# Row passes two fetches behind, every second one-hot on VectorE, and 64 expert chunks ahead instead of 80

## The chip, the cores and the metric

The kernel runs on one core of a Trainium2 chip. The metric is the device time in microseconds (us) from the start to the end of one execution; a median over several executions is quoted. The engines are called TensorE (PE in the rows, PEld for its weight loads), VectorE (DVE), ScalarE (ACT), GpSimd (POOL) and SyncE (SP, which issues most DMAs). Each engine runs its own list of instructions strictly in order and waits on semaphores for the others.

## The reference, cut to what matters

One layer of a decoder trunk over 512 tokens of width 2048, in float32. A mixer (sparse attention and a Mamba-2 scan) comes first and is not touched. After it stands PEER, a retrieval over 16384 one-neuron experts: each token picks 16 experts for each of 8 heads, 128 in all, and adds up what they give.

```python
v1, i1 = lax.top_k(s1, 16); v2, i2 = lax.top_k(s2, 16)      # s1, s2: scores of 128 + 128 keys
best, pos = lax.top_k(cand, 16)                             # cand: the 256 sums v1 + v2
eidx = take_along_axis(i1 * 128 + i2, pos); gate = softmax(best)
act = gelu(einsum('td,tkd->tk', h, u_tab[eidx]))            # 128 rows of u for each token
ffn = einsum('tk,tkd->td', act * gate, v_tab[eidx])         # 128 rows of v for each token
```

`u_tab` and `v_tab` are 16384 x 2048, 128 MB each.

## The kernel before, in words

The 512 tokens of PEER are split between two ways of computing the same thing.

- **352 tokens the dense way.** All experts are computed for these tokens, and a matrix G of gates, zero for experts that a token did not pick, is multiplied in. The experts come in 128 chunks of 128. A *u chunk* (`uchunk`, L826) loads 1 MB of `u` in two halves. `wsplit` (L241) brings each half (`wr`), lets ScalarE round it (`wh`, L248) and VectorE take the rest (`wl`, L249); the pools have 3 buffers of each. TensorE then does 48 matmuls of 352 columns (L253 to L255, three for a product), and ScalarE applies gelu (`ac`, L835). A *v group* (`vgroup`, L1057) is the same with `v` for 8 chunks: 16 halves, and VectorE adds each result into `outT` (L1075, L1077).
- **160 tokens by rows.** GpSimd fetches, in 320 steps of 1 MB, one row of 2048 for each of 128 partitions (`rows`, L950, 3 buffers). VectorE makes a *row pass* over each: a dot product with h for the 160 rows of `u` (L955), then a multiply-add into `facc` for the 160 of `v` (L964, L971). `gather_step` (L945) writes the fetch and its pass one behind the other. `pace` (L977) sets when the fetches go: each u chunk counts one unit of work, each of the 16 halves of a v group half a unit, 256 in all; for each unit 333/256 = 1.3 fetches become due, and each waits for the instruction that ended the unit.

The order of the stages, with the lines that matter:

1. *Routing.* VectorE finds the top 16 (`route`, L855). After each of the 8 heads `go_ahead` (L984) writes 4 u chunks (`NA_TOPK`) whose `ac` goes to DRAM (`ascr`) for later.
2. *G.* For 11 blocks of 32 tokens, 8 banks of 4 tokens each: VectorE makes `oa` (L1015), the one-hot of the first key; ScalarE makes `ob`, the one-hot of the second key times the gate, in two activations (L1020, L1021; 8 buffers); TensorE multiplies them (L1022), and ScalarE copies the bank out to `stg` (L1023). After each block `go_ahead` writes `NA_G` = 4 u chunks, and after the last block what is left of the `NA` = 80.
3. *Groups.* The 16 groups of 8 chunks. `wgroup` (L1035) makes the weights of v: for chunks below `NA` it loads `ac` back from `ascr`, the others are computed there. `vgroup` follows. The list `order` puts a group that is still to be computed before one that is ready: with 80 ahead 10, 0, 11, 1, ... 15, 5, and then 6, 7, 8, 9.
4. *End.* The last groups' sums, the 160 tokens' transposes, the final norm.

What the kernel writes is not what an engine runs. A scheduler lays each engine's list out from the written order: of the instructions that it takes to be ready at a time it takes the first written, and `wsplit`'s two go ahead of all others (`tc.high_priority`). So the place of a row pass in VectorE's list is set by both.

Of the kernel before, what the change touches and what calls it, by code (L numbers as in the profile page):

```python
# [13 lines left out]
AF = mybir.ActivationFunctionType  # L14
ALU = mybir.AluOpType
# [10 lines left out]
NB = 384 - ND  # L26
QB = 128 // NB
GRP = 8
NA = 80
NA_TOPK = 4  # L30
NA_G = 4
UAB = 4
WB = 12
ADA_SSM = (0, 0, 1, 1, 2, 2, 2, 2)
# [121 lines left out]
def build(tc, nc, I, out, dbg=None, stop=None):  # L156
    dbg = dbg or {}
    es = ExitStack()
    V, S, PE, G, SP = nc.vector, nc.scalar, nc.tensor, nc.gpsimd, nc.sync
# [20 lines left out]
    iota = cst[:, C_IOTA:C_IOTA + 128]  # L180
# [35 lines left out]
    for hf in range(2):  # L216
        ct = adp.tile([128, 1024], F32, name="ct", tag="at", bufs=3)
        sl = slice(1024 * hf, 1024 * hf + 1024)
# [4 lines left out]
    def after_(ins, first):  # L223
        if first is not None:
            tc.add_manual_dep(ins.ins, first.ins.name,
                              mybir.DependencyInfo(mybir.DependencyClass.Sync, mybir.DependencyReason.DATA), reason="pace")
# [114 lines left out]
    with ExitStack() as sx:  # L341
# [80 lines left out]
        for g in range(2):  # L422
# [7 lines left out]
            for c in range(4):  # L430
                sl = slice(128 * c, 128 * c + 128)
# [7 lines left out]
        for p in range(8):  # L439
# [17 lines left out]
            for j in range(2):  # L457
                for c in range(4):
                    V.tensor_scalar(M[:, j, c], R[:, j, 128 * c:128 * c + 128], acst[:, c, 2 * p + j:2 * p + j + 1], 0.0,
                                    op0=ALU.subtract, op1=ALU.min)  # L460
# [13 lines left out]
            for c in range(4):  # L474
                sl = slice(128 * c, 128 * c + 128)
# [6 lines left out]
                if c < 3:  # L482
# [5 lines left out]
                    else:  # L488
                        for j in range(2):
                            V.scalar_tensor_tensor(Sn[:, 64 * j:64 * j + 64], St[:, 64 * j:64 * j + 64],  # L490
                                                   eal[:, j, c:c + 1], su[:, 64 * j:64 * j + 64],
                                                   op0=ALU.mult, op1=ALU.add)
# [28 lines left out]
    with ExitStack() as sx:  # L521
# [10 lines left out]
        with tc.tile_pool(name="mlp", bufs=1) as mp:  # L532
# [9 lines left out]
            for c0, n in ((0, 512), (512, 128)):  # L542
# [3 lines left out]
                                       op0=ALU.mult, op1=ALU.add)  # L546
            SP.dma_start(rvscr, rv.unsqueeze(1).to_broadcast([16, 128, 640]))
            for which in range(2):
# [33 lines left out]
                if which == 0:  # L582
# [3 lines left out]
                    for k in range(2):  # L586
                        sl = slice(NCMP * k, NCMP * k + NCMP)
# [43 lines left out]
        for h in range(NH):  # L631
# [4 lines left out]
            if h == 14:  # L636
                mH, mL = act_tiles()
                for k in range(0, 8, 2):
                    m = st.tile([128, 1024], F32, name="wr", tag="wr")
                    SP.dma_start(m.rearrange("p (a b) -> p a b", a=2), yscr[k:k + 2].rearrange("a p b -> p a b"))  # L640
                    for c in range(2):
                        sl = slice(T * c, T * c + T)
# [20 lines left out]
            for br in range(3):  # L663
                for i in range(4):
# [8 lines left out]
                    if br == 0:  # L673
                        bias = TB[:, 415 - 128 * i:415 - 128 * i + 16 * (n - 1) + 1:16]
                    else:
                        bias = TB[:, 384 - 128 * i:384 - 128 * i + n]
                    V.tensor_tensor_reduce(out=P, in0=sps[:, :n], in1=bias, scale=1.0, scalar=3e38, op0=ALU.add,
                                           op1=ALU.min, accum_out=mn[:, ki:ki + 1])
# [141 lines left out]
    I2T = ixp.tile([128, ND], F32, name="I2T")  # L820
# [121 lines left out]
    steps = [("u", 0, sl) for sl in range(128)] + [("u", 1, sl) for sl in range(NB)] + \  # L942
        [("v", 0, sl) for sl in range(128)] + [("v", 1, sl) for sl in range(NB)]

    def gather_step(s, after):  # L945
        nonlocal facc, faccb
        side, grp, sl = steps[s]
        rows = gp.tile([128, D], F32, name="rows", tag="rows", bufs=3)
        ei = eidxb if grp else eidx
        ins = G.indirect_dma_start(out=rows, out_offset=None, in_=I["un"] if side == "u" else I["vn"],  # L950
                                   in_offset=bass.IndirectOffsetOnAxis(ap=ei[:, sl:sl + 1], axis=0))
        after_(ins, after)
        c = 128 * grp + sl
        if side == "u":
            V.scalar_tensor_tensor(rows, rows, 1.0, h2b if grp else h2t, op0=ALU.mult, op1=ALU.mult,  # L955
                                   accum_out=dots[:, c:c + 1])
            n = NB if grp else 128
            if sl == n - 1:
                gs_ = slice(128 * grp, 128 * grp + n)
                S.activation(wgt[:, gs_], dots[:, gs_], AF.Gelu_apprx_tanh)  # L960
                V.tensor_tensor(wgt[:, gs_], wgt[:, gs_], ggateb if grp else ggate, op=ALU.mult)
        elif sl == 0:
            f = gp.tile([128, D], F32, name="facc", tag="faccb" if grp else "facc")
            V.tensor_scalar(f, rows, wgt[:, c:c + 1], None, op0=ALU.mult)  # L964
            if grp:
                faccb = f
            else:
                facc = f
        else:
            f = faccb if grp else facc  # L970
            V.scalar_tensor_tensor(f, rows, wgt[:, c:c + 1], f, op0=ALU.mult, op1=ALU.add)  # L971
# [5 lines left out]
    def pace(units, after):  # L977
        nonlocal gdone, work
        work += units
        while gdone < min(len(steps), G0 + (GEND - G0) * work / total):  # L980
            gather_step(gdone, after)
            gdone += 1

    def go_ahead(n):  # L984
        for _ in range(n):
# [22 lines left out]
    with tc.tile_pool(name="gstage", bufs=1, side="right") as sp:  # L1008
        for tq in range(ND // 32):
            stg = sp.tile([128, 128, 32], F32, name="stg", tag="stg", bufs=2)  # L1010
            for t4 in range(8):
                gb = next(gbank)()
                t0 = 32 * tq + 4 * t4
                oa = sp.tile([128, 4, 128], F32, name="oa", tag="oa", bufs=3)
                V.tensor_tensor(oa, iota.unsqueeze(1).to_broadcast([128, 4, 128]),  # L1015
                                I1T[:, t0:t0 + 4].unsqueeze(2).to_broadcast([128, 4, 128]), op=ALU.is_equal)
                for k in range(4):
                    t = t0 + k
                    ob = sp.tile([128, 128], F32, name="ob", tag="ob", bufs=8)
                    S.activation(ob, iota, AF.Square, bias=I2N[:, t:t + 1])  # L1020
                    S.activation(ob, ob, AF.Relu, scale=GTN[:, t:t + 1], bias=GTT[:, t:t + 1])  # L1021
                    PE.matmul(gb[:, 128 * k:128 * k + 128], ob, oa[:, k], start=True, stop=True)  # L1022
                S.copy(stg[:, :, 4 * t4:4 * t4 + 4].rearrange("p a t -> p t a"),  # L1023
                       gb.rearrange("p (t a) -> p t a", t=4))
            SP.dma_start(gscr[tq], stg)
            go_ahead(NA_G)
    go_ahead(NA)
# [115 lines left out]
```

## Time and profile before

| what | us |
|---|---|
| median of 3 runs | 3595.86 (3570.61 to 3595.88) |
| the profiled execution | 3587.35 |
| its span, first to last instruction | 3585.6 |
| TensorE busy | 3210.6 (90%) |
| VectorE busy | 2685.9 (75%) |
| ScalarE busy | 1526.0 (43%) |
| GpSimd busy | 489.7 (14%) |

The profile gives instructions with start and duration, and for each wait of an engine what released it. Busy is the sum of durations without overlaps. Matmuls are pipelined, so their durations overlap and the step from one start to the next is what one costs; the same holds, less strongly, for ScalarE and VectorE. PEclk is the share of TensorE's full clock (2.4 GHz) that was granted. DMA share is the mean busy share of the 16 DMA engines. A bank here is the work on 4 tokens of G: one `oa`, four `ob`, four products, one copy.

### The profile page before, as it was taken

Reading aid. Unit: us, or ns where it says so; the run is one execution under the profiler, and the core shown is the slowest. Engines: PE = TensorE matmul, PEld = TensorE weight load, DVE = VectorE, ACT = ScalarE, POOL = GpSimd, SP = SyncE. Lnnn points to the kernel's source line nnn. Section 1 sums busy time; section 2 is a strip of 40 time slices with the busy share of each in tenths; the row PEclk is TensorE's granted clock in tenths of the full one; section 3 lists DMA queues with packets and bytes.
Section 4 is the critical chain, followed back from the end, with each engine's and each line's share of the span. In section 5 each row is a group of like instructions: output and inputs, shape, how many; then the busy total and the mean of one; then the engine's idle time right before and its main releaser. Section 6 shows DMA issues by size and latency. Waiting matters only on the chain. (4 is left out here: it accounts for less than half of the span.)

```text
span 3585.6 us, 48243 instructions
## 1 busy us (share of the span) xinstructions
PE 3210.6 (90%) x18025; PEld 2942.0 (82%) x18025; DVE 2685.9 (75%) x4567; ACT 1526.0 (43%) x2775; POOL 489.7 (14%) x324
## 2 busy tenths in 40 slices
PE   5999679999899999868888999999898989988897
PEld 3777568878677999858777999989898989988897
DVE  8888479977777999725554577777777768777786
ACT  3443247962432434498777432323222232322222
POOL 0000000000000112101011122322322222232220
PEclk9999889999899999969899999999999999999999
DMA  9647884238522888736676788898888888798884
GB/s 345 245 160 236 187 270 137 76 107 283 191 88 93 283 299 328 274 125 241 251 275 249 294 317 299 309 320 321 303 289 313 307 301 310 280 319 303 309 313 144
DMA packets 292666, 905.02 MB, mean 252 GB/s; under 512 B 24064, under 2 KB 89856, under 8 KB 249264
## 3 DMA queue, kind: packets, MB, share of 16 engines
q1 hardware_dynamic: 246352, 566.39, 47.0%
q0 software_dynamic: 46080, 335.56, 24.3%
q8 instruction: 141, 2.31, 0.3%
q14 instruction: 93, 0.76, 0.1%
HBM read 845.46 MB, written 56.39 MB: 252 GB/s over the span
## 5 line engine op out<-in xcount | busy, mean ns | idle before, releaser
L248 ACT CAST wh<-wr 128x1024 fp32r<-128x1024 f32 x646 | 676.1, 1049 | 1196.2 <-DMA wr<-in_ut_dram 251.1
L249 DVE TENSOR_TENSOR wl<-wr,wh 128x1024 fp32r<-128x1024 f32 x646 | 786.9, 1221 | 194.9 <-ACT wh L248 180.9
L255 PE MATMUL mm<-dh,wl 128*128 128x352 f32 x2048 | 682.9, 333 | 44.4 <-DVE wl L249 44.0
L253 PE MATMUL mm<-dh,wh 128*128 128x352 f32 x2048 | 678.2, 331 | 1.0 <-ACT wh L248 1.0
L254 PE MATMUL mm<-dl,wh 128*128 128x352 f32 x2048 | 675.6, 330 | 0.0
L971 DVE SCALAR_TENSOR_TENSOR facc<-rows,wgt,facc 128x2048 f32<-128x2048 f32 x158 | 371.3, 2350 | 172.4 <-DMA rows<-in_vn_dram,eidx 147.5
L255 PEld LDWEIGHTS mm<-dh,wl 128*128 128x128 f32 x2048 | 395.1, 193 | 55.2 <-DVE wl L249 54.8
L950 POOL DMA_INDIRECT rows<-in_un_dram,eidx x128 | 159.4, 1245 | 2049.9 <-DMA wr<-in_ut_dram 1183.1
L253 PEld LDWEIGHTS mm<-dh,wh 128*128 128x128 f32 x2048 | 394.3, 193 | 1.6 <-ACT wh L248 1.6
L254 PEld LDWEIGHTS mm<-dl,wh 128*128 128x128 f32 x2048 | 394.7, 193 | 0.0
L955 DVE SCALAR_TENSOR_TENSOR rows<-rows,h2t 128x2048 f32<-128x2048 f32 x128 | 292.6, 2286 | 131.2 <-DMA rows<-in_un_dram,eidx 131.2
L253 PE MATMUL mm<-ah,wh 128*128 128x512 f32 x864 | 344.0, 404 | 5.5 <-DVE rr__7022 L287 3.1
L254 PE MATMUL mm<-al,wh 128*128 128x512 f32 x864 | 346.0, 401 | 0.0
L255 PE MATMUL mm<-ah,wl 128*128 128x512 f32 x864 | 345.0, 400 | 0.0
L950 POOL DMA_INDIRECT rows<-in_vn_dram,eidx x128 | 220.7, 1724 | 630.8 <-ACT ac L835 198.9
L236 DVE SCALAR_TENSOR_TENSOR at<-at,cond 128x1024 f32<-128x1024 f32 x192 | 231.4, 1221 | 41.6 <-DMA at<-in_ada_dram 41.1
L253 PEld LDWEIGHTS mm<-ah,wh 128*128 128x128 f32 x864 | 164.8, 191 | 40.9 <-issue 5.5
L254 PEld LDWEIGHTS mm<-al,wh 128*128 128x128 f32 x864 | 164.8, 191 | 34.2 <-issue 3.0
L255 PEld LDWEIGHTS mm<-ah,wl 128*128 128x128 f32 x864 | 164.3, 190 | 34.7 <-issue 3.0
L1021 ACT ACTIVATE ob<-ob,GTT,GTN 128x128 f32<-128x128 f32 x352 | 155.2, 486 | 0.0
L1015 DVE TENSOR_TENSOR oa<-cst,I1T 128x512 f32<-128x512 f32 x88 | 59.8, 690 | 121.2 <-PE t L1022 52.1
L1020 ACT ACTIVATE ob<-cst,I2N 128x128 f32<-128x128 f32 x352 | 121.6, 393 | 0.0
(2961 smaller groups left out, 6588.1 us busy)
## 6 DMA issues: line engine op xcount, KB each, us to landing
wr<-in_ut_dram SPq DMA_DIRECT2D x256, 512.0 KB, 5.5
wr<-in_vn_dram SPq DMA_DIRECT2D x256, 512.0 KB, 6.3
at<-in_ada_dram SPq DMA_DIRECT2D x192, 512.0 KB, 5.7
wr<-in_win_dram SPq DMA_DIRECT2D x54, 512.0 KB, 4.9
gscr<-stg SPq DMA_DIRECT2D x11, 2048.0 KB, 12.5
gt<-gscr SPq DMA_DIRECT2D x32, 704.0 KB, 8.8
wr<-in_wo_dram SPq DMA_DIRECT2D x32, 512.0 KB, 5.2
wr<-in_wq_dram SPq DMA_DIRECT2D x32, 512.0 KB, 3.8
```

The lines of the kernel that those rows point to most:

```text
L236: V.scalar_tensor_tensor(at, at, 1.0, cond[:, sl], op0=ALU.mult, op1=ALU.mult, accum_out=acc[:, hf, k:k + 1])
L248: S.copy(hi[:, :n], raw[:, :n])
L249: V.tensor_tensor(lo[:, :n], raw[:, :n], hi[:, :n].bitcast(F32), op=ALU.subtract)
L253: PE.matmul(acc, wh, ah, start=start, stop=False)
L254: PE.matmul(acc, wh, al, start=False, stop=False)
L255: return PE.matmul(acc, wl, ah, start=False, stop=stop)
L950: ins = G.indirect_dma_start(out=rows, out_offset=None, in_=I["un"] if side == "u" else I["vn"], in_offset=bass.IndirectOffsetOnAxis(ap=ei ...
L955: V.scalar_tensor_tensor(rows, rows, 1.0, h2b if grp else h2t, op0=ALU.mult, op1=ALU.mult, accum_out=dots[:, c:c + 1])
L971: V.scalar_tensor_tensor(f, rows, wgt[:, c:c + 1], f, op0=ALU.mult, op1=ALU.add)
L1015: V.tensor_tensor(oa, iota.unsqueeze(1).to_broadcast([128, 4, 128]), I1T[:, t0:t0 + 4].unsqueeze(2).to_broadcast([128, 4, 128]), op=ALU.is ...
L1020: S.activation(ob, iota, AF.Square, bias=I2N[:, t:t + 1])
L1021: S.activation(ob, ob, AF.Relu, scale=GTN[:, t:t + 1], bias=GTT[:, t:t + 1])
```

## The change

Three edits. `gather_step` is cut into `fetch` and `use_rows`, and a row pass is written only when two more fetches have been written (`LAG` = 2). Of the four `ob` of a bank the first and third are made by VectorE in one instruction, an `is_equal` with one per-partition scalar and a `mult` with another; the second and fourth stay on ScalarE. And `NA` falls from 80 to 64 with `NA_G` from 4 to 3, so 16 u chunks move from the G stage into the groups, whose order becomes 8, 0, 9, 1, ... 15, 7.

```diff
-NA = 80
+NA = 64
 NA_TOPK = 4
-NA_G = 4
+NA_G = 3
+LAG = 2
...
-    def gather_step(s, after):
-        nonlocal facc, faccb
+    fetched = []
+
+    def fetch(s, after):
         side, grp, sl = steps[s]
         rows = gp.tile([128, D], F32, name="rows", tag="rows", bufs=3)
...
         after_(ins, after)
+        fetched.append((side, grp, sl, rows))
+
+    def use_rows():
+        nonlocal facc, faccb
+        side, grp, sl, rows = fetched.pop(0)
         c = 128 * grp + sl
...
         while gdone < min(len(steps), G0 + (GEND - G0) * work / total):
-            gather_step(gdone, after)
+            fetch(gdone, after)
             gdone += 1
+            if len(fetched) > LAG:
+                use_rows()
+        while gdone == len(steps) and fetched:
+            use_rows()
...
-                    S.activation(ob, iota, AF.Square, bias=I2N[:, t:t + 1])
-                    S.activation(ob, ob, AF.Relu, scale=GTN[:, t:t + 1], bias=GTT[:, t:t + 1])
+                    if k % 2:
+                        S.activation(ob, iota, AF.Square, bias=I2N[:, t:t + 1])
+                        S.activation(ob, ob, AF.Relu, scale=GTN[:, t:t + 1], bias=GTT[:, t:t + 1])
+                    else:
+                        V.tensor_scalar(ob, iota, I2T[:, t:t + 1], GTT[:, t:t + 1], op0=ALU.is_equal, op1=ALU.mult)
```

How the lists of the engines change is shown at three places. The number at a row's start is its place in the engine's list, L the line of that kernel (the changed one has 13 or 14 lines more there).

ScalarE in the G stage, two banks (`stg` is the copy that ends a bank), before:

```order
1298 L1023 COPY stg<-t 128x4x128
1299 L1021 ACTIVATE ob<-ob,GTT,GTN 128x128
1300 L1020 ACTIVATE ob<-cst,I2N 128x128 x2
1301 L1021 ACTIVATE ob<-ob,GTT,GTN 128x128 x2
1302 L1020 ACTIVATE ob<-cst,I2N 128x128 x2
1303 L1021 ACTIVATE ob<-ob,GTT,GTN 128x128 x2
1304 L1020 ACTIVATE ob<-cst,I2N 128x128
1305 L1023 COPY stg<-s 128x4x128
1306 L1021 ACTIVATE ob<-ob,GTT,GTN 128x128
1307 L248 CAST wh<-wr 128x1024
```

and of the changed kernel, with the gelu of a u chunk (`ac`) among them:

```order
1193 L1037 COPY stg<-t 128x4x128
1194 L1032 ACTIVATE ob<-cst,I2N 128x128
1195 L836 ACTIVATE ac<-mm 128x352
1196 L1033 ACTIVATE ob<-ob,GTT,GTN 128x128
1197 L1032 ACTIVATE ob<-cst,I2N 128x128 x2
1198 L1033 ACTIVATE ob<-ob,GTT,GTN 128x128
1199 L1037 COPY stg<-s 128x4x128
1200 L1033 ACTIVATE ob<-ob,GTT,GTN 128x128
1201 L1032 ACTIVATE ob<-cst,I2N 128x128 x2
1202 L1037 COPY stg<-t 128x4x128
```

Between two copies there stood eight activations and now there stand four.

VectorE in the G stage (`wl` is a half of a u chunk, `rows` a row pass), before:

```order
2520 L1015 TENSOR_TENSOR oa<-cst,I1T 128x512 x2
2521 L249 TENSOR_TENSOR wl<-wr,wh 128x1024
2522 L1015 TENSOR_TENSOR oa<-cst,I1T 128x512
2523 L249 TENSOR_TENSOR wl<-wr,wh 128x1024
2524 L1015 TENSOR_TENSOR oa<-cst,I1T 128x512
2525 L249 TENSOR_TENSOR wl<-wr,wh 128x1024
2526 L955 SCALAR_TENSOR_TENSOR rows,dots<-rows,h2t 128x2048
2527 L249 TENSOR_TENSOR wl<-wr,wh 128x1024
```

and of the changed kernel:

```order
2479 L1026 TENSOR_TENSOR oa<-cst,I1T 128x512 x2
2480 L250 TENSOR_TENSOR wl<-wr,wh 128x1024
2481 L1035 TENSOR_SCALAR ob<-cst,I2T,GTT 128x128 x3
2482 L962 SCALAR_TENSOR_TENSOR rows,dots<-rows,h2t 128x2048
2483 L1035 TENSOR_SCALAR ob<-cst,I2T,GTT 128x128 x2
2484 L1026 TENSOR_TENSOR oa<-cst,I1T 128x512 x2
2485 L962 SCALAR_TENSOR_TENSOR rows,dots<-rows,h2t 128x2048
2486 L250 TENSOR_TENSOR wl<-wr,wh 128x1024
```

The one-hots now stand behind row passes and halves of u chunks in the same list.

VectorE in the groups. The numbers behind the names are given as the kernel is written out, so a `wl` with a higher number than a `rows` belongs to weights that are written after that row's fetch. Before:

```order
3015 L249 TENSOR_TENSOR wl_21984<-wr_21981,wh_21983 128x1024
3016 L1049 TENSOR_TENSOR ac_21894<-ac_21894,gt_21615 128x352
3017 L1052 TENSOR_TENSOR wl__21900<-ac_21894,wh__21899 128x352
3018 L249 TENSOR_TENSOR wl_22014<-wr_22011,wh_22013 128x1024
3019 L971 SCALAR_TENSOR_TENSOR facc_21305<-rows_21896,wgt_10325,facc_21305 128x2048
3020 L249 TENSOR_TENSOR wl_22055<-wr_22052,wh_22054 128x1024
3021 L1049 TENSOR_TENSOR ac_21967<-ac_21967,gt_21904 128x352
3022 L1052 TENSOR_TENSOR wl__21976<-ac_21967,wh__21975 128x352
3023 L249 TENSOR_TENSOR wl_22085<-wr_22082,wh_22084 128x1024
3024 L971 SCALAR_TENSOR_TENSOR facc_21305<-rows_21969,wgt_10325,facc_21305 128x2048
```

and of the changed kernel:

```order
3252 L250 TENSOR_TENSOR wl_22011<-wr_22008,wh_22010 128x1024
3253 L250 TENSOR_TENSOR wl_22044<-wr_22041,wh_22043 128x1024
3254 L978 SCALAR_TENSOR_TENSOR facc_21267<-rows_21934,wgt_10325,facc_21267 128x2048
3255 L250 TENSOR_TENSOR wl_22081<-wr_22078,wh_22080 128x1024
3256 L250 TENSOR_TENSOR wl_22111<-wr_22108,wh_22110 128x1024
3257 L1091 TENSOR_TENSOR o12_10313<-o12_10313,t_21941 128x352
3258 L1091 TENSOR_TENSOR o13_10314<-o13_10314,t_21942 128x352
3259 L1091 TENSOR_TENSOR o14_10315<-o14_10315,o_21943 128x352
3260 L978 SCALAR_TENSOR_TENSOR facc_21267<-rows_22005,wgt_10325,facc_21267 128x2048
```

Before, `rows_21969` is passed over behind four halves with higher numbers (21984, 22014, 22055, 22085); in the changed kernel `rows_22005` also stands behind four (22011, 22044, 22081, 22111).

## Rows read from the trace of the kernel before

**Rows 1.** Busy time of the engines by stage: routing, the G stage, the rest of the chunks ahead, the groups. The columns are the stretch in us, its length, PE, PEld, DVE, ACT and POOL busy with the number of instructions, PEclk, DMA share, GB/s.

```profile
1190.00:1505.00 315.00, 299.11 (x1816) 292.32 (x1815) 297.29 (x631) 123.13 (x180) 63.25 (x48) 0.98 0.84 315
1505.00:2000.00 495.00, 402.84 (x2338) 374.62 (x2339) 235.13 (x243) 397.20 (x889) 44.73 (x44) 0.86 0.58 219
2000.00:2052.00 52.00, 47.28 (x282) 46.42 (x281) 30.73 (x27) 14.97 (x19) 9.71 (x9) 0.97 0.99 370
2052.00:3510.00 1458.00, 1348.55 (x8150) 1332.48 (x8149) 1121.14 (x1143) 423.75 (x517) 368.45 (x217) 0.97 0.86 307
```

**Rows 2.** ScalarE's and VectorE's groups of instructions from 1505 to 2000 us, shapes apart: out<-in, shapes, count | busy us, mean ns | idle just before, and what ended it.

```profile
L248 ACT CAST wh<-wr 128x1024 fp32r<-128x1024 f32 x68 | 71.3, 1048 | 71.4 <-DMA wr<-in_ut_dram 68.7 <-PE mm L254 2.2
L835 ACT ACTIVATE ac<-mm 128x352 f32<-128x352 f32 x35 | 14.9, 451 | 0.0
L955 DVE SCALAR_TENSOR_TENSOR rows<-rows,h2t 128x2048 f32<-128x2048 f32 x43 | 98.4, 2288 | 78.4 <-DMA rows<-in_un_dram,eidx 78.4
L249 DVE TENSOR_TENSOR wl<-wr,wh 128x1024 fp32r<-128x1024 f32 x69 | 84.3, 1222 | 58.3 <-ACT wh L248 58.3
L1015 DVE TENSOR_TENSOR oa<-cst,I1T 128x512 f32<-128x512 f32 x88 | 59.8, 690 | 121.2 <-PE t L1022 52.1 <-PE s L1022 48.5 <-PE o L1022 20.6
```

**Rows 3.** ScalarE in order of time, in one block of the G stage: start, us, engine, line, operation, tiles, count, and idle time before it with its releaser.

```profile
1767.14 1.04 ACT L248 CAST wh<-wr 128x1024 fp32r<-128x1024 f32 x1 [10.10 <-DMA wr<-in_ut_dram]
1768.09 0.46 ACT L835 ACTIVATE ac<-mm 128x352 f32<-128x352 f32 x1
1768.45 1.05 ACT L1023 COPY stg<-t 128x512 f32<-128x512 f32 x1
...
1785.11 1.12 ACT L1023 COPY stg<-s 128x512 f32<-128x512 f32 x1
1786.01 0.86 ACT L1021 ACTIVATE ob<-ob,GTT,GTN 128x128 f32<-128x128 f32 x2
1786.77 0.68 ACT L1020 ACTIVATE ob<-cst,I2N 128x128 f32<-128x128 f32 x2
1787.36 0.87 ACT L1021 ACTIVATE ob<-ob,GTT,GTN 128x128 f32<-128x128 f32 x2
1788.25 1.05 ACT L248 CAST wh<-wr 128x1024 fp32r<-128x1024 f32 x1
1789.21 1.14 ACT L1023 COPY stg<-t 128x512 f32<-128x512 f32 x1
```

**Rows 4.** VectorE in the same block, in order of time.

```profile
1760.01 2.29 DVE L955 SCALAR_TENSOR_TENSOR rows<-rows,h2t 128x2048 f32<-128x2048 f32 x1 [8.81 <-DMA rows<-in_un_dram,eidx]
...
1762.23 1.22 DVE L249 TENSOR_TENSOR wl<-wr,wh 128x1024 fp32r<-128x1024 f32 x1
```

**Rows 5.** Busy time as in Rows 1, for the start of the G stage and for the two halves of that block.

```profile
1505.00:1569.00 64.00, 44.71 (x203) 36.83 (x204) 17.82 (x23) 59.19 (x142) 0.00 (x0) 0.68 0.21 74
1747.00:1768.00 21.00, 16.27 (x106) 15.69 (x105) 9.92 (x9) 10.90 (x24) 4.00 (x4) 0.96 0.95 364
1768.00:1798.00 30.00, 26.16 (x154) 24.75 (x154) 15.96 (x18) 27.68 (x63) 0.99 (x1) 0.85 0.42 156
```

**Rows 6.** TensorE in order of time, where products of one-hots (L1022, two instructions each) stand among the 352-column matmuls of a u chunk.

```profile
1740.35 0.49 PE L1022 MATMUL t<-oa,ob 128*128 128x128 f32 x2 [0.33 <-ACT ob L1021]
1740.60 0.41 PE L254 MATMUL mm<-dl,wh 128*128 128x352 f32 x1
1740.84 0.38 PE L1022 MATMUL t<-oa,ob 128*128 128x128 f32 x2
1740.98 0.41 PE L255 MATMUL mm<-dh,wl 128*128 128x352 f32 x1
1741.23 0.32 PE L253 MATMUL mm<-dh,wh 128*128 128x352 f32 x1
1741.39 0.32 PE L254 MATMUL mm<-dl,wh 128*128 128x352 f32 x1
```

**Rows 7.** An instruction of VectorE of the form of the new one-hot (128 x 128 float32, per-partition scalars), over the whole span, columns as in Rows 2.

```profile
L459 DVE TENSOR_SCALAR M<-R,acst 128x128 f32<-128x128 f32 x64 | 15.0, 282 | 0.0
```

**Rows 8.** The gelu at the end of each u chunk in the groups, one row for a group of 8 (the first row has the last chunk ahead too), four of the six groups, with the fastest and the slowest among them: durations min/median/max, and the start of the first and the last.

```profile
L835 ACT ACTIVATE ac<-mm x9: 449/454/458, 2051.9 to 2120.1; 128x352 f32<-128x352 f32 x9
L835 ACT ACTIVATE ac<-mm x8: 450/454/458, 2463.9 to 2517.2; 128x352 f32<-128x352 f32 x8
L835 ACT ACTIVATE ac<-mm x8: 449/454/459, 2664.0 to 2724.6; 128x352 f32<-128x352 f32 x8
L835 ACT ACTIVATE ac<-mm x8: 449/452/462, 2869.9 to 2930.9; 128x352 f32<-128x352 f32 x8
```

**Rows 9.** Waits in the groups, 2052 to 3510 us: the engine and line that waited <- what released it: us in total, times, longest.

```profile
DVE facc L971 <- DMA rows<-in_vn_dram,eidx: 147.5, 66, 8.2
PE t L253 <- DVE o L1077: 32.7, 13, 7.1
PE s L253 <- DVE o L1077: 21.2, 11, 6.3
PE s L255 <- DVE wl L249: 15.2, 6, 5.3
PE mm L255 <- DVE wl L249: 13.2, 5, 3.8
```

**Rows 10.** The fetches: GpSimd's time to issue them in the whole span (as in Rows 2).

```profile
L950 POOL DMA_INDIRECT rows<-in_un_dram,eidx x128 | 159.4, 1245 | 2049.9 <-DMA wr<-in_ut_dram 1183.1
```

## The prediction

> **What bounds the kernel now.** I read the busy times by stage first [rows 1]. Four stages follow the mixer, and each has another limit. In routing VectorE is busy 297 of 315 us: what VectorE does sets the end, and 39 of the 80 chunks ahead run beside it. In the G stage (495 us, 35 chunks and 88 banks) no engine looks full: TensorE 403, ScalarE 397, VectorE 235. Then come the last 6 chunks ahead, with the DMA engines 99% busy. In the groups (1458 us) TensorE is busy 1349 and the DMA engines 86%: near both limits, with small waits.
>
> A mean that shows no full engine asks for a look inside. The first 64 us of the G stage hold no end of a chunk and ScalarE works 59 of them, TensorE at a granted clock of 0.68 [rows 5]. Later blocks have two halves. From 1768 to 1798 ScalarE is busy 27.7 of 30 us while the DMA engines are at 42%: ScalarE is the limit. From 1747 to 1768 it is the other way, DMA 95% at 364 GB/s and ScalarE half idle [rows 5]. Why, the order of time tells: VectorE stands 8.8 us before a row pass whose rows have not landed [rows 4], the halves `wl` behind it can't be made, their `wr` buffers stay full, and ScalarE waits 10.1 us for the next `wr` [rows 3]. So a block of 8 banks and 4 chunks costs 50 us: some 30 by ScalarE, some 20 by fetches and loads that come all at once.
>
> **The one-hots.** What one thing costs is the step between starts. On ScalarE: two one-hots from 1786.01 to 1787.36, 0.68 us each; a bank's copy 1785.11 to 1786.01, 0.90; a half chunk's `wh` 1788.25 to 1789.21, 0.96; a gelu 1768.09 to 1768.45, 0.36 [rows 3]. A bank is 4 x 0.68 + 0.90 = 3.6 us before and 2 x 0.68 + 0.90 = 2.26 after; a chunk 2 x 0.96 + 0.36 = 2.28. On TensorE a 352-column matmul steps 0.16 (1741.23 to 1741.39), so a chunk is 48 x 0.16 = 7.7 us; two products of one-hots and two such matmuls take 0.88 (1740.35 to 1741.23), so a product is 0.28 and a bank 1.1 [rows 6].
>
> VectorE's new instruction is not in the trace, but its form is: 128 x 128 float32 with per-partition scalars takes 282 ns [rows 7]. So 176 of them are 50 us at most; VectorE has 260 us free in the G stage [rows 1]. What they cost beyond that is that they stand in VectorE's list behind row passes and halves, as the second place of the order shows. The nearest row is the 8.8 us wait [rows 4]; nothing if the rows have landed.
>
> By the Trainium skill (SBUF — State Buffer, Who interferes with whom) a tensor_scalar with float32 in SBUF can run in a mode that takes the port pair which GpSimd needs to write its DMA descriptors, and GpSimd is blocked until it ends. No row here has such instructions beside fetches; a fetch takes GpSimd 1.25 us as it is [rows 10]. By that rule some 30 fetches of the G stage (23 chunks x 1.3) would each start up to 0.28 us later, 8 us together if all of it showed, where the sum below has nothing.
>
> **The G stage after.** The changed order has 39 chunks before the first one-hot, as before, and 23 before the last copy instead of 35. It spreads them: 15 chunks among the first 64 banks, one for 4.3 banks, where before 16 banks passed without any. Then 24 banks and 8 chunks follow in three blocks in the old manner, two chunks in a run of 98 matmuls and then 8 banks.
>
> Spread part: ScalarE 64 x 2.26 + 15 x 2.28 = 179 us. TensorE 64 x 1.1 + 15 x 7.7 = 187. VectorE, by durations [rows 2, 7]: 64 x (0.69 + 0.56) + 15 x (2 x 1.22 + 1.3 x 2.29) = 161. Two engines near the same sum: I take 187 / 0.92 = 203 us, since ScalarE in its own half was busy 92% (27.7 of 30). Ends: 179 if ScalarE alone counts; 231 if TensorE is busy no more than now (187 x 495 / 403).
>
> Blocks: 8 banks and half a chunk's work on ScalarE, 8 x 2.26 + 2 x 0.96 = 20 us; the run of two chunks 15.4 us by TensorE, 21 as before [rows 5]. I take 18: three times 38 = 114. Ends 106 and 123.
>
> G stage 203 + 114 = 317 us, from 1505 to 1822; the last two chunks ahead 16 more, so 64 are ready at 1838.
>
> **The 16 chunks that move.** In the groups a chunk steps 7.6 to 8.7 us, over the four groups shown 8.4 [rows 8]. 16 x 8.4 = 134 (122 to 139). So 80 chunks' worth is reached at 1838 + 134 = 1972; before, it was at 2052. That is 80 us less. The moved chunks give back most of what the G stage sheds (2052 - 1838 = 214).
>
> **The row passes.** The groups have the waits that the edit names: VectorE waits 147 us for rows of v alone, and TensorE waits for VectorE behind it, 82 us in the four largest rows [rows 9]. But in VectorE's list the passes stay where they were. Counting in the whole list how many halves `wl` written after a row's fetch stand ahead of its pass, it is 4 for 197 and 5 for 13 of the last 210 passes before, 193 and 17 after; the third place of the order shows both. A pass goes in when the scheduler takes its rows to be there, whether it is written two fetches later or not, and `wsplit`'s halves go first either way. I cost this edit at nothing in the groups. In routing, passes do move back by one half in the mean, and 49 instead of 51 stand ahead of the first `oa`: 2 x 2.29 us leave a stage that VectorE bounds and go where it has room. Between -5 and +5 us, since the third buffer's next fetch then waits longer; I take 0. The 16 `ac` that no longer go through DRAM are 32 DMAs of 176 KB, 5.8 MB or 18 us at the groups' 307 GB/s [rows 1]; they lie under TensorE's work, with the DMA engines at 86%. I count nothing, 18 us less at most.
>
> **The sum.** 3587 us is the profiled execution's own time; less 80 it is 3507. The median of the runs shown is 8.5 us above that execution, so 3596 - 80 = 3516 us. Ends of the terms together: 179 + 106, with chunks at 7.6, gives 2052 - (1505 + 285 + 16 + 122) = 124 less, 3472; 231 + 123 with 8.7 gives 2052 - (1505 + 354 + 16 + 139) = 38 less, 3558.
>
> **Rivals.**
>
> *The passes do move in time.* The lists say no, but the lists are not the times: spread chunks and other fetches could let rows land before their pass in the groups too. Then the 82 us of TensorE's waits go, at most: 3516 - 82 = 3434, half of it 3475. For it speaks that the waits are real; against it that 4 halves ahead is what the waits of before came from. 0.12.
>
> *A wash.* The two engines of the spread part do not overlap as ScalarE alone did: each bank needs `ob` from both, so a delay on either holds TensorE, and the G stage takes 354 to 400 us. Break-even is 2052 - 1505 - 16 - 134 = 397. For it speaks that three lists are now within 187 to 161 us of each other; against it that the order of the list mixes products and matmuls finely, so TensorE can work on a chunk between. 3560 to 3600. 0.18.
>
> *Slower: one-hots behind a row pass that waits.* Before, ScalarE made all `ob` and ran on while VectorE stood at a pass; now half of them are behind it, and a wait of VectorE stops TensorE and the copies as well. Place: the 15 + 3 chunks of the G stage that release fetches; price 8.8 us each [rows 4], 158 us on the 285 of the lower ends: 443, which is 46 over the 397 from which it decides, 3642. For it speaks that the passes stand 4 halves behind as before. Against it: the 8.8 us stood behind three fetches released at once, and 15 of the chunks are now 13 us apart with one or two fetches each; VectorE's wait for rows in the whole stage was 78 us [rows 2]. 0.08.
>
> **How the numbers follow.** Forecast 0.62, of which 0.05 lies above 3560. One per cent, 36 us, is about what a measurement of this kernel can tell from no change: faster is below 3560, slower above 3632. Faster: 0.57 + 0.12 + 0.03 of the wash's lower edge = 0.72; within 1%: 0.05 + 0.15 = 0.20; slower 0.08. The range leaves out the slower rival and the far half of the first: 3455 to 3595.
>
> **What would show it.** Right: the G stage ends near 1822, its first 64 banks with an `ac` every 13 us and a granted clock above 0.68; ScalarE's waits for `wr` of 10 us three times and not some seven (68.7 us in all [rows 2]); new one-hots of some 0.28 us; chunks in the groups still at 8.4 us and VectorE's waits for rows of v there still near 2.2 us each (147.5 / 66). Wrong: a G stage over 380 us (then look for TensorE's waits on VectorE's `ob`); chunks in the groups above 9 us, if DMA has become the limit there; or rows that have landed before every pass.

## The result and the profile after

The changed kernel takes 3463.75 us (median of 4, 3454.46 to 3476.76) against 3583.24 us of the kernel before (median of 4, 3563.58 to 3595.88): ratio 0.9674, 95% interval 0.9605 to 0.9742. The forecast was 3516 us with a range of 3455 to 3595. Direction, mechanism and range held; the time is 52 us shorter than said.

Stages of the two profiled executions in us. A stage begins and ends with an instruction: routing from the cast of `eidx` to the first product of one-hots, G to the last copy to `stg`, the tail to the gelu of the last chunk ahead, the groups to the end.

| | routing | G | tail | groups | end |
|---|---|---|---|---|---|
| before | 322.9 | 494.2 | 52.3 | 1533.6 | 3585.5 |
| after | 311.8 | 332.9 | 8.8 | 1637.5 | 3470.7 |
| difference | -11.1 | -161.3 | -43.5 | +103.9 | -114.8 |
| forecast | 0 | -178 | -36 | +134 | -80 |

(The last column also holds 2.8 us from ahead of routing.) The windows of the trace after, columns as in [rows 1]: routing, G, the first 64 us of G, its first 64 banks (TensorE ends the last product of them at 1702), its last three blocks, a burst and the 20 us behind it, the groups up to the last gelu, and the rest.

```profile
1180.00:1491.00 311.00, 293.87 (x1782) 287.69 (x1783) 299.29 (x652) 120.03 (x173) 68.74 (x51) 0.98 0.85 317
1491.50:1824.50 333.00, 292.74 (x1833) 270.60 (x1833) 228.57 (x373) 258.32 (x509) 42.83 (x30) 0.95 0.68 249
1491.50:1555.50 64.00, 60.06 (x394) 54.48 (x394) 51.77 (x87) 58.33 (x116) 8.80 (x6) 1.00 0.71 257
1491.50:1702.00 210.50, 190.62 (x1207) 173.63 (x1207) 154.34 (x264) 182.43 (x364) 28.66 (x18) 0.97 0.69 252
1702.00:1824.50 122.50, 102.12 (x628) 96.97 (x627) 74.23 (x109) 75.89 (x147) 14.17 (x12) 0.92 0.66 245
1746.00:1766.00 20.00, 13.90 (x93) 13.71 (x91) 10.73 (x11) 5.86 (x10) 2.17 (x3) 0.94 0.98 368
1766.00:1786.00 20.00, 19.37 (x113) 17.64 (x114) 14.69 (x28) 18.95 (x39) 1.74 (x1) 0.89 0.34 120
1833.00:3311.00 1478.00, 1392.23 (x8462) 1373.21 (x8461) 1136.95 (x1124) 440.43 (x539) 347.79 (x229) 0.98 0.88 311
3311.00:3470.00 159.00, 133.48 (x816) 131.37 (x814) 116.00 (x161) 45.66 (x59) 16.99 (x9) 0.92 0.63 221
```

The first 64 us of G had a granted clock of 0.68 and no end of a chunk [rows 5]; now they have 1.00, and over the first 64 banks the clock is 0.97 and TensorE is busy 191 of 210 us. One burst of the old kind is left in each late block (1746 to 1766: DMA engines at 98%, ScalarE busy 6 of 20 us), and right behind it ScalarE is full again.

What waits in G after, 1490 to 1830 us, groups of instructions as in [rows 2]:

```profile
L249 ACT CAST wh<-wr 128x1024 fp32r<-128x1024 f32 x49 | 51.7, 1056 | 49.1 <-DMA wr<-in_ut_dram 17.9 <-PE mm L255 15.1 <-PE s L1036 8.1
L962 DVE SCALAR_TENSOR_TENSOR rows<-rows,h2t 128x2048 f32<-128x2048 f32 x32 | 73.3, 2290 | 44.0 <-DMA rows<-in_un_dram,eidx 44.0
L1035 DVE TENSOR_SCALAR ob<-cst,I2T,GTT 128x128 f32<-128x128 f32 x176 | 54.2, 346 | 0.0
L1036 PE MATMUL s<-oa,ob 128*128 128x128 f32 x288 | 55.3, 300 | 17.5 <-DVE ob L1035 14.3 <-ACT ob L1033 2.4
```

ScalarE's waits for loads fell from 68.7 [rows 2] to 17.9 us. A new wait has come: TensorE stands for VectorE's `ob` (14.3 us in this row, 8.7 and 8.4 in the two other banks of PSUM, 31 together), and ahead of it VectorE stands at rows that have not landed, 44.0 us. That is the mechanism of the rival on the slower side, at a fifth of its price. In the first 64 banks TensorE's part of it is 12.6 us. Nearly all of the rest is one wait of 5.5 to 6.1 us in each late block, where VectorE stands 6.6 to 7.1 us at a row pass. The first of them:

```profile
1715.68 2.29 DVE L962 SCALAR_TENSOR_TENSOR rows<-rows,h2t 128x2048 f32<-128x2048 f32 x1 [7.11 <-DMA rows<-in_un_dram,eidx]
...
1725.76 0.79 PE L1036 MATMUL t<-oa,ob 128*128 128x128 f32 x2 [6.14 <-DVE ob L1035]
```

Waits in the groups after, 1838 to 3370 us, columns as in [rows 9]:

```profile
DVE facc L978 <- DMA rows<-in_vn_dram,eidx: 130.3, 71, 6.6
DVE rows L962 <- DMA rows<-in_un_dram,eidx: 49.5, 26, 8.0
PE t L254 <- DVE o L1091: 21.0, 13, 6.6
PE s L254 <- DVE o L1091: 17.5, 11, 5.4
PE mm L256 <- DVE wl L250: 17.0, 13, 4.0
PE o L256 <- DVE wl L250: 11.8, 3, 5.3
```

The waits that "two fetches later" names are still there: 130 us for rows of v against 147 [rows 9]. The passes were written later and ran where they ran before.

### The profile page after: what moved, and what is told of

Its sections match the earlier page's. It is cut to its first block, busy times and chain, and to the rows that moved or that the text cites. A ratio compares the mean times of both kernels' runs of the same rounds, so it can differ in the third digit from the quotient of the medians.

```text
span 3470.6 us, 47955 instructions
## 1 busy us (share of the span) xinstructions
PE 3175.1 (91%) x18025; PEld 2908.8 (84%) x18025; DVE 2733.2 (79%) x4743; ACT 1411.8 (41%) x2423; POOL 478.0 (14%) x324
## 4 chain that ended last, share of the span: by engine, by line
PE 29%; issue 25%; DMA 22%; DVE 17%; POOL 4%; ACT 3%; another core or an unknown queue 1%; SPq 0%; POOLq 0%; DVEq 0%; ACTq 0%
DMA rows<-in_un_dram,eidx 6%; DMA rows<-in_vn_dram,eidx 6%; PE mm L254 5%; PE mm L256 5%; PE mm L255 5%; DVE wl L250 4%; POOL rows L952 4%; DVE at L237 2%; DMA ac<-ascr 2%; DMA rows<-in_vn_dram,eidxb 2%; DVE facc L978 2%; DVE rows L962 2%; DMA wr<-in_vn_dram 2%; DMA rows<-in_un_dram,eidxb 1%; PE s L254 1%
## 5 line engine op out<-in xcount | busy, mean ns | idle before, releaser
L952 POOL DMA_INDIRECT rows<-in_un_dram,eidx x128 | 182.7, 1427 | 1938.3 <-DMA wr<-in_ut_dram 1180.4
L952 POOL DMA_INDIRECT rows<-in_vn_dram,eidx x128 | 200.1, 1563 | 628.6 <-ACT ac L836 208.6
L962 DVE SCALAR_TENSOR_TENSOR rows<-rows,h2b 128x2048 f32<-128x2048 f32 x32 | 73.3, 2290 | 28.0 <-DMA rows<-in_un_dram,eidxb 27.8
L1063 DVE TENSOR_TENSOR ac<-ac,gt 128x352 f32<-128x352 f32 x128 | 65.2, 522 | 32.4 <-DMA ac<-ascr 32.1
```

The lines of the kernel that those rows point to most:

```text
L1063: V.tensor_tensor(ac.rearrange("p (q t) -> p q t", t=32), ac.rearrange("p (q t) -> p q t", t=32), gt[:, :, 32 * k4:32 * k4 + 32], op=ALU.mult)
```

## The experiments

Every ratio is to the kernel before on the same chip (its medians there: 3578 to 3586 us), with its 95% interval. Stages in us as above.

| kernel | median | ratio | routing | G + tail | groups |
|---|---|---|---|---|---|
| onehot_only | 3506.5 | 0.979 [0.9757, 0.9824] | 322.2 | 478.6 | 1515.1 |
| na_only | 3573.0 | 0.9976 [0.9951, 1.0001] | 319.6 | 409.6 | 1630.4 |
| lag_only | 3563.5 | 0.994 [0.9917, 0.9963] | 313.0 | 549.0 | 1520.3 |
| no_lag | 3490.2 | 0.9747 [0.9705, 0.9789] | 323.4 | 340.4 | 1638.0 |
| ahead80 | 3486.6 | 0.9719 [0.9652, 0.9786] | 313.9 | 474.2 | 1508.5 |
| ahead48 | 3475.8 | 0.9701 [0.9625, 0.9777] | 310.7 | G 272.8 | |
| start_late | 3499.5 | 0.9743 [0.9673, 0.9812] | 256.1 | 421.6 | 1654.2 |
| stt_onehot | 3473.2 | 0.9665 [0.9594, 0.9736] | 314.2 | 342.0 | 1644.5 |
| spread | 3466.2 | 0.9667 [0.962, 0.9714] | 311.1 | 326.6 | 1643.2 |
| held2 | 3381.8 | 0.9419 [0.9378, 0.946] | 312.4 | 329.6 | 1563.0 |
| spread_held2 | 3358.4 | 0.9364 [0.9323, 0.9405] | 312.4 | 303.1 | 1564.6 |
| held_only | 3489.2 | 0.9723 [0.9649, 0.9798] | 313.4 | 542.4 | 1448.8 |

(The 48th chunk of ahead48 ends inside G, so its last columns have no counterpart. In na_only, spread and spread_held2 the gelu of the last chunk ahead comes 0.3, 4 and 9 us before G's last copy, so there "G + tail" ends that much before G does.)

### Which edit does it

**onehot_only**: the kernel before with the new one-hots alone.

> Every second one-hot on VectorE, the rest as before (80 chunks ahead, passes written behind their fetch). If ScalarE's relief is the gain and the number ahead a trade, the G stage, still with 35 chunks, is bound by TensorE: 88 x 1.12 + 35 x 7.7 = 368 us, say 395 against 494, and the total 3583 - 100 = 3485 (0.972). If the moved chunks are what brings it, the stage keeps its bursts of fetches at 21 us a block and stays near 440, total 3530 (0.985). If row passes bring it: no more than 20 us (0.995).

Two thirds of the gain: G goes from 494 to 419 us. That falls short of what was expected (395 us, 0.972): VectorE waits 87 us for rows in this stage, and TensorE 48 us for VectorE's `ob` (1490 to 1950 us). na_only and no_lag below differ in the one-hots alone as well, and there the ratio falls by as much, from 0.9976 to 0.9747. The tail, which the DMA engines bound [rows 1], stays (52 and 59).

**na_only**: the kernel before with the two numbers alone.

```diff
-NA = 80
+NA = 64
-NA_G = 4
+NA_G = 3
```

> 64 chunks ahead instead of 80, all one-hots on ScalarE, passes written behind their fetch. By ScalarE's relief: ScalarE bounds the G stage, 88 x 3.62 + 23 x 2.28 = 371 us, say 400 against 494; the tail of 52 us falls to 10; the groups take 104 us more, as measured in the changed kernel: total 3583 - 94 - 43 + 104 = 3550 (0.991). If the moved chunks are cheap in the groups by themselves: 3520 or less (0.982).

G and tail lose 137 us, the groups gain 97, and over all executions the time stays at 0.9976 (the profiled one was the fastest of its ten). The move is a trade.

**lag_only**: the kernel before with `fetch`, `use_rows` and `LAG = 2` alone.

> Only the row passes written two fetches later. If VectorE's list is what counts: routing, from the last index of the rows to the first product of G, falls from 323 to some 312 us as in the changed kernel, the groups stay at 1534, total 0.997 (3572). If passes come late enough in time everywhere: VectorE's waits for rows in the groups (147 us for rows of v) fall by more than half and the total is 0.98. If the 11 us of routing were chance: 1.000.

Small, but the interval leaves out 1: 0.994. Half of it is routing, 322.9 to 313.0. VectorE's waits for rows in that stage, before and here:

```profile
DVE rows L955 <- DMA rows<-in_un_dram,eidx: 9.7, 9, 2.7
```

```profile
DVE rows L962 <- DMA rows<-in_un_dram,eidx: 4.1, 7, 1.1
```

and its busy time (the fifth column), before and here:

```profile
1182.00:1505.00 323.00, 302.41 (x1827) 295.50 (x1826) 305.12 (x661) 124.17 (x181) 66.62 (x51) 0.98 0.84 312
```

```profile
1177.00:1490.00 313.00, 295.39 (x1782) 289.41 (x1782) 300.69 (x656) 120.78 (x176) 66.57 (x51) 0.97 0.85 316
```

4.4 us less work (49 passes ahead of the first `oa`, not 51) and 5.6 us less waiting: VectorE bounds this stage, so both count in full. In the groups the waits for rows of v are 128 us (147 in [rows 9]), and of the last 210 passes 197 stand behind 4 halves and 13 behind 5, as before. The groups are 13 us shorter in this execution all the same.

**no_lag**: the changed kernel with `LAG = 0`, so without that edit.

> The changed kernel with passes written right behind their fetch again. If the lag is worth the 11 us of routing: 3464 + 11 = 3475, 0.970 of before, with routing back at 323 us and G and groups as in the changed kernel (333 and 1637). If it is worth nothing: 0.967. If the lag is what brings a good part: 0.98 or more.

Routing is back at 323.4; G, tail and groups are within 2 us of the changed kernel's. So in this pair the lag does nothing in the groups. Three pairs of kernels differ in the lag alone (before and lag_only, onehot_only and ahead80, no_lag and the changed kernel), and in each the ratio is lower with it, by 0.006 or 0.007. Routing is 8 to 12 us of that, about half. The groups differ by 13, 7 and 0.5 us, so no stage has the other half in all three, and its cause is open. The three ratios alone multiply to 0.979 x 0.9976 x 0.994 = 0.9708, inside the interval of all three together.

### How many chunks ahead

**ahead80**: the changed kernel with `NA = 80`, `NA_G = 4`. **ahead48**: with `NA = 48`, `NA_G = 1`.

> The changed kernel with 80 chunks ahead and 4 a block again, so one-hots and lag alone. If edits add up: 0.979 x 0.994 = 0.973 of before, routing 312 us, G 419, tail 57, groups 1518. If fewer chunks ahead is needed for the rest to pay: 0.98 or more. If it is worth nothing: 0.967.

> The changed kernel with 48 chunks ahead, 1 a block. If a chunk costs in the groups what TensorE takes for it, the G stage is now bound by ScalarE (88 x 2.26 + 8 x 2.28 = 217, say 235 us against 333, with TensorE at a lower granted clock) and the groups take 16 x 7.0 = 112 more: 3464 + 14 = 3478 (0.971). If the G stage has other waits that the chunks hid: 0.98. If fewer ahead is better without end: 0.96.

0.972, 0.967, 0.970 for 80, 64, 48 chunks: no difference that these intervals tell. What G sheds the groups take: from ahead80 to the changed kernel G and tail lose 133 us and the groups gain 129. ahead80 came as the sum of the edits has it. For ahead48 the total did (0.971 was expected), its G stage did not: 273 us and not 235.

**start_late**: the changed kernel with `G0 = -20` for 0, so that the fetches begin 20 later against the work and routing holds 23 passes and not 49.

> The changed kernel with the fetches set later (G0 = -20 instead of 0, the end as before): 23 row passes instead of 49 stand in VectorE's list ahead of the first one-hot of G. If VectorE bounds routing, 26 passes x 2.29 = 60 us leave it, until TensorE (294 busy of 311) is the limit: routing 312 to some 290, and passes find room later: 3464 - 20 = 3444 (0.961). If what leaves routing comes back in the groups, where the DMA engines are 88% busy and now fetch 6% more a unit: 0.967 to 0.972, with the groups 20 to 40 us longer.

The time lies above both expectations. Routing falls by 56 us as VectorE has less to do, but only 32 chunks are done when G starts, not 39, and G grows by 82 us. Some 62 of these are work of TensorE that came along (busy 355 us in G, not 293). The rest is near what its waits for VectorE's `ob` rise by, from 31 to 54 us (1440 to 1860 us):

```profile
PE s L1036 <- DVE ob L1035: 24.1, 4, 7.3
PE t L1036 <- DVE ob L1035: 20.9, 5, 5.6
PE o L1036 <- DVE ob L1035: 9.0, 2, 5.0
```

The chunks are the larger part of it. The longer waits go with more row passes in G, 43 and not 32, which the one-hots stand behind.

### The form of the one-hot

**stt_onehot**: the same product in another instruction.

```diff
-                        V.tensor_scalar(ob, iota, I2T[:, t:t + 1], GTT[:, t:t + 1], op0=ALU.is_equal, op1=ALU.mult)
+                        V.scalar_tensor_tensor(ob, iota, I2T[:, t:t + 1], GTT[:, t:t + 1].to_broadcast([128, 128]),
+                                               op0=ALU.is_equal, op1=ALU.mult)
```

> The changed kernel with VectorE's one-hots as scalar_tensor_tensor, the gate read as a broadcast tensor, so an instruction with two tensors from SBUF. If the tensor_scalar form holds GpSimd up while it writes descriptors, a fetch in the G stage takes GpSimd 1.0 to 1.1 us to issue again instead of 1.4; the time stays 0.967, since a fetch has 4 halves of slack. If the length of the one-hot counts on VectorE, the total goes with it, 88 x 2 x its change.

GpSimd's fetches from 1505 to 1820 us, in before, after, no_lag, stt_onehot and held_only (described further down; all its one-hots are on ScalarE):

```profile
L950 POOL DMA_INDIRECT rows<-in_un_dram,eidx x27 | 27.7, 1024 | 297.2 <-ACT ac L835 245.9 <-DVE rows L955 48.3 <-issue 1.2
```

```profile
L952 POOL DMA_INDIRECT rows<-in_un_dram,eidx x28 | 39.0, 1393 | 264.9 <-ACT ac L836 156.4 <-DVE ob L1035 63.3 <-DVE rows L962 25.4
```

```profile
L952 POOL DMA_INDIRECT rows<-in_un_dram,eidx x28 | 32.0, 1142 | 285.7 <-ACT ac L836 210.7 <-DVE ob L1035 50.5 <-DVE wl L250 12.1
```

```profile
L952 POOL DMA_INDIRECT rows<-in_un_dram,eidx x28 | 37.6, 1342 | 263.5 <-ACT ac L836 223.6 <-DVE rows L962 16.1 <-DVE ob L1035 13.4
```

```profile
L952 POOL DMA_INDIRECT rows<-in_un_dram,eidx x28 | 47.8, 1709 | 271.8 <-ACT ac L836 224.2 <-DVE rows L962 42.2 <-ACT ob L1031 3.4
```

A fetch takes longer to issue in the changed kernel, 1.39 us for 1.02, 28 x 0.37 = 10 us in all, near the estimate of 8 us from the Trainium skill (SBUF — State Buffer, Who interferes with whom). But these runs don't show that rule as the cause: the other form of the one-hot costs nearly as much (1.34, where 1.0 to 1.1 was expected), the same form 1.14 in no_lag, and held_only, with no one-hot on VectorE, 1.71. What sets it is open, and the time is the same, 0.9665 and 0.9674.

### Bursts, and passes that truly run later

**spread**: a chunk is written behind banks 2, 5 and 8 of a block, not three behind the block.

```diff
+                if t4 % 3 == 1:
+                    go_ahead(1)
...
-            go_ahead(NA_G)
```

> The changed kernel, but the three u chunks of a block of G are written one behind each of its banks 2, 5 and 8 instead of all three behind the block, so that the order has a chunk every 2 to 3 banks up to the end and no run of two chunks. Theory (what is left over the sum of TensorE's work in the G stage comes from the blocks at its end, where two or three chunks in a row with their loads and fetches fill the DMA engines at 98% while TensorE is busy 14 of 20 us): the 20 us stretches with TensorE at 14 go, G stage and tail 342 us in the changed kernel become 316 to 322, the groups stay within 10 us of 1637; time 20 to 25 us under the changed kernel, 0.960 to 0.962 of before. Rival (the bursts are only where the DMA engines work off what the stage owes them, 249 GB/s in the mean): the stage stays within 8 us of 342, and the time within 8 us of the changed kernel, 0.965 to 0.970.

The theory fell. To the gelu of the last chunk ahead G and tail came down by 15 us, not 20 to 26, and G itself, to its last copy, only from 333 to 331. The median did not come down (3466 and 3464), as the rival had it. ScalarE's and VectorE's longest waits in G, 1490 to 1830 us:

```profile
ACT wh L249 <- DMA wr<-in_ut_dram: 3.5, 1, 3.5
...
DVE rows L962 <- DMA rows<-in_un_dram,eidx: 60.6, 17, 7.4
...
PE t L1036 <- DVE ob L1035: 11.8, 5, 4.1
PE s L1036 <- DVE ob L1035: 11.4, 5, 3.8
PE o L1036 <- DVE ob L1035: 4.8, 3, 3.6
```

The waits for loads are nearly gone (17.9 to 3.5 us), the ones for rows have grown (44.0 to 60.6), and TensorE still stands 28 us for `ob`. So the bursts were not the root. That the passes stand too early is what the next run tests.

**held2**: each row pass also waits for the instruction that ended the unit of work in which it is written (`pace` hands `after` on), so the scheduler can't place it sooner. Of the last 210 passes 140 now stand behind 5 halves and 65 behind 6 to 8, where 193 stood behind 4 (the "4 for 140" of the expectation should be 5).

```diff
-    def use_rows():
+    def use_rows(after=None):
...
-            V.scalar_tensor_tensor(f, rows, wgt[:, c:c + 1], f, op0=ALU.mult, op1=ALU.add)
+            after_(V.scalar_tensor_tensor(f, rows, wgt[:, c:c + 1], f, op0=ALU.mult, op1=ALU.add), after)
...
-                use_rows()
+                use_rows(after)
```

(and the same `after_` around the two other passes)

> The changed kernel, but each row pass also waits for the instruction that ended the unit of work in which it is written, so it stands behind 5 to 7 halves in VectorE's list in the groups (4 for 140, 6 for 25, 7 for 39 of the last passes) and not 4. Theory (the row passes' place in the list, not the order in which they are written, decides whether rows have landed): VectorE's waits for rows of v in the groups, 130 us for those released by indices and 50 us for the others in the changed kernel, fall by 30 to 60%, TensorE's waits for VectorE there (some 75 us in the largest rows) fall by 15 to 40 us, and the time goes 10 to 30 us under the changed kernel. Rival 1 (the three buffers of rows bind: a pass that runs later lets the third fetch after it start later, and the rows land as much later): the waits stay within 20% and so does the time, within 8 us. Rival 2 (a pass that is held makes VectorE wait for TensorE where it had work): the waits change their name, and the time is 10 to 40 us over the changed kernel.

84 us under spread on the same chip and 82 under the changed kernel's median, three to eight times what the theory said. Its waits in the groups, 1838 to 3370 us:

```profile
DVE wl L250 <- ACT wh L249: 179.7, 110, 5.8
...
DVE facc L978 <- DMA rows<-in_vn_dram,eidx: 6.1, 5, 2.1
...
PE s L254 <- DVE o L1091: 11.8, 5, 6.7
PE t L254 <- DVE o L1091: 10.0, 7, 3.0
PE s L256 <- DVE wl L250: 7.8, 5, 3.8
```

130 us became 6, and TensorE's waits for VectorE, 91 us in after (its nine largest rows), became 36. VectorE now idles 180 us before its halves because ScalarE has not rounded them yet, but TensorE hardly feels it: its rows of waits for `wl` were 45.5 us in after and are 7.8 here. One to three halves more were enough, so the three buffers of rows were not what bound. The groups lose 74.5 us, more than the 55 of these waits; the granted clock in the groups also rises, from 0.98 to 0.99 (1838 to 3360 us). How the rest splits is open.

**spread_held2**: both edits.

> Both of the two edits before: chunks of G one behind banks 2, 5 and 8 of a block, and row passes held to the unit in which they are written. If the two are independent the time is the sum of what each gives alone. By the theories for both 30 to 55 us under the changed kernel, 0.952 to 0.960 of before; by the rivals within 10 us of the changed kernel, or over it.

Busy time in its G stage, and TensorE's only row of waits for `ob` of VectorE there:

```profile
1489.00:1800.50 311.50, 293.39 (x1925) 272.02 (x1924) 237.40 (x380) 265.13 (x514) 54.61 (x33) 1.00 0.77 281
```

```profile
PE s L1036 <- DVE ob L1035: 1.6, 1, 1.6
```

The best version: 3358 us, 0.9364. The edits are not independent: spreading is worth nothing alone (+2 us) and 23 us once the passes are held. In G no wait of VectorE for rows is among its seven largest, TensorE waits 1.6 us for `ob` and is granted its full clock. Theory and rivals all put it slower than it is.

**held_only**: the kernel before with the lag and the hold, and nothing else.

> The kernel before with one edit alone: row passes written two fetches late, and each of them waiting for the instruction that ended the unit of work in which it is written. The one-hots stay on ScalarE and 80 chunks stay ahead. In the groups the passes then stand behind 5 to 7 halves. Theory (what the changed kernel's lag lacked is the hold, and the hold is worth the same without the other two edits): VectorE's waits for rows of v fall from 147 us to under 20, TensorE's waits for VectorE in the groups from some 100 us to under 50, and the groups' 1534 us fall by 50 to 80; the G stage, where ScalarE sets the pace, loses its 10 us waits for loads and comes down from 494 to 440 to 480. Together 80 to 110 us less, 0.970 to 0.978. Rival 1 (the hold pays only where 64 and not 80 chunks are ahead, as more of the row traffic then lies beside u chunks): 20 to 50 us less, 0.986 to 0.994. Rival 2 (ScalarE waits for VectorE's held halves in the G stage of before): the groups gain and the G stage gives it back, within 20 us of before.

The total is as the theory has it, 0.9723, the split is not. The groups lose 85 us (1533.6 to 1448.8), a little over the 50 to 80, and TensorE's waits for VectorE there fall from 109 to 47 us (2052 to 3440 us). G loses 3 and not 14 to 54: ScalarE's waits there, 1500 to 2000 us, have partly changed their name:

```profile
ACT wh L249 <- DVE wl L250: 37.5, 4, 9.6
ACT wh L249 <- DMA wr<-in_ut_dram: 27.6, 3, 9.4
```

Together 65 us, where the loads alone took 68.7 [rows 2]. Whether the hold does it without the lag was not run: all three held kernels have both.

## Why the prediction was right, and where its sizes were off

**The one-hots: right.** G was ScalarE's, and half its one-hots elsewhere shorten it. Alone they are worth 2.1% (onehot_only); the clock in the first 64 us went from 0.68 to 1.00, with a gelu every 14 us in the first 64 banks (16 from 1499 to 1704; 13 were said), and ScalarE's waits for loads are four, 17.9 us, not the 68.7 of before. The instruction takes 346 ns, not 282. `M<-R` [rows 7] was the nearest row, but not of the same form: it reads one per-partition scalar and a constant (L459), the new instruction two such scalars. 11 us over 176 is what it missed, in a stage where VectorE had room.

**The G stage: 333 us for 317, in the bounds of 285 to 354.** Both parts were a little longer than said. The first 64 banks took 210.5 us for 203. TensorE was busy 190.6 of it, where 187 were worked out, and that is 91%, where I took 92. It stood 12.6 for VectorE's `ob` (three rows, 7.7 the largest). The three late blocks took 122.5 for 114, just inside the upper end of 123. The run of two chunks that opens each took 16 us, less than the 18 that I took. But behind each run TensorE stood 5.5 to 6.1 us for `ob`, since VectorE stood at a row pass. This wait is the term that the sum put at nothing, and over the stage it is 31 us. (The upper end of the first part, 231 in the text, is 230 by its own numbers.)

**The rival on the slower side: its place was right, its price wrong.** 18 waits of 8.8 us were put on TensorE. VectorE waited 17 times for rows in G, 44 us in all, and TensorE 31 us for `ob`, ten times; start_late, with more passes in G, shows 54, and onehot_only, with 35 chunks in G, 48.

**The 16 chunks: 104 us for 134.** I priced them at the step of a u chunk in the groups, 8.4 us [rows 8]. But when 16 chunks move, `order` changes too: four ready groups leave the end, where they ran alone, for the alternation. The gelus mark both. Before, from 2052 to 3136, 48 u chunks and the v of 10 groups take 1084 us, 8.47 a chunk (128 chunks of u or v); after, 64 and 14 groups from 1833 to 3311, 1478 us, 8.40. The rest up to the end is 450 us before with 6 groups and 160 after with 2: 72.5 a group, or 9.06 a chunk. So 16 x 8.4 = 134, less 32 x (9.06 - 8.40) = 21, less 128 x 0.07 = 9, is 104. This is the account of one pair of executions. ahead80 and the changed kernel differ in the two numbers alone, and the same account (1065 us for ahead80's alternation, 443.5 for its rest) gives 134 - 15 + 10 = 129 there. So the gain of the four groups shows in both (21 and 15 us), the last term has either sign, and 16 chunks cost 97 us (before and na_only) to 129 us in the groups: the forecast's 134 is closer than the 30 us suggest.

**The lag: right in the groups, wrong in routing.** "They stay where they were" held: the waits for rows of v are 130 us, and with the lag taken out the groups are the same (1638.0 and 1637.5). In routing the passes do move, as the text said, and I then took 0 from -5 to +5; it is -11. I had counted the two passes that leave (4.6 us) and cancelled them against a supposed wait of the third buffer. The waits for rows fell as well, by 5.6.

**The rival that passes move in time** did not happen in this kernel. Its price was near: 82 us at most were said, and where the passes are made to move the groups give 85 (held_only) and 75 us (held2). Part of that is luck, since TensorE's waits for VectorE, from which the 82 came, fell by 62 and 55 us.

Of the 52 us that the forecast lies too high, 30 are the chunks in this pair of executions, 5 the earlier 64th chunk (1833 for 1838: G's 16 us too many against routing's 11, the tail's 7 and the 3 ahead of routing), and 17 the offset: the profiled execution was 8.5 us under the median before, and after it is 8.7 above. That the misses around the 64th chunk nearly cancel is luck.

## What to carry to other kernels

Writing an instruction later need not make it run later where a scheduler fills each engine's list (in the groups here it did not): look where it stands, and give it a dependence if it has to stand elsewhere. On an engine that works in order a wait is paid by whoever needs what is queued behind it, so take that wait away before work is moved onto that engine or a burst is spread. Price moved work by the rates of the place it leaves and the place it goes to, and ask what else moves along.

## What the runs showed that was not expected

- How little a pass has to move: one to three halves more ahead of it (some 4 us each) take VectorE's waits for rows of v from 130 to 6 us, with the same three buffers and the same traffic (DMA share 0.88 and 0.89, 312 and 318 GB/s from 1838 to 3360 us).
- One 128 x 128 one-hot on VectorE takes 346 ns with two per-partition scalars and 345 with a broadcast tensor in place of the second, where `M<-R`, with one such scalar and a constant, takes 282 [rows 7].
- Issuing a fetch takes GpSimd 1.02 us in G before (1505 to 1820 us) and 1.10 to 1.76 in the other kernels that have one-hots on VectorE or held passes. The time does not follow it: held2 and spread_held2, the two fastest, have 1.76 and 1.65.
